# Eight of eleven down-projection steps by seven products, with a second weight sum formed early and kept in DRAM

## The chip, the core and the metric

The kernel runs on one core of one Trainium2 chip. Its engines run in parallel, each with an instruction stream of its own: TensorE (PE, with PEld for its weight loads), VectorE (DVE), ScalarE (ACT), GpSimd (POOL) and SyncE (SP, which here only issues DMAs). They meet through semaphores. The metric is device microseconds of one launch, the median of the runs shown. Weights come from DRAM by DMA and are multiplied out of on-chip tiles; sums stand in PSUM.

## The reference

One decoder layer on 16 meta tokens and 256 tokens of width 2048, in float32. The mixing part (8 retention heads, 4 mLSTM heads) is not touched by the change. What follows it is:

```python
mix = jnp.concatenate([ret, hm], axis=-1) @ w_out          # 2048 x 2048
h = h + mix
u = rmsnorm(h, norm_ffn)
up = causal_dwconv(u @ w_up, ffn_conv_w, ffn_conv_b)       # 2048 x 11264, 3 taps
gate, val = jnp.split(up, [FFN_DIM], axis=-1)              # FFN_DIM = 5632
return h + (jax.nn.silu(gate) * val) @ w_down              # 5632 x 2048
```

After it comes a last RMS norm, and the meta tokens are dropped.

## The kernel before

**Precision.** Each operand of a product is kept as a high part (float32r, a cast on ScalarE, `whi`, `sh`, `mh`) and a low part (the rest, a subtraction on VectorE, `wlo`, `sl`, `ml`). One product is three matmuls: high by high, low activation by high weight, high activation by low weight. `split` (line 763) makes both parts of a tile.

**Stages.** Input projection and heads, output projection (lines 640 to 648, 16 tiles of 128 columns in halves), then twice an up projection of 22 pairs of tiles (gate and value, lines 769 to 810) followed by the down projection of this half of the 5632 channels (lines 913 to 957). A half has `NQD` = 11 steps `q` of two channel tiles each. The 2048 output columns are four blocks of 512, taken in two pairs: `b` = 0 and 2. So there are four passes of 11 steps, one for each half and pair.

**Plain steps.** For a step and a pair the 256 tokens (two tiles) meet two channel tiles and two column blocks: eight products, done by `product` (line 814) with weights from `load_step`, into the PSUM tiles `cs[tt, j]`.

**Steps by seven products.** Steps in `FAST` do the same as a 2 x 2 block product with seven products (Winograd's form). Write the activation blocks as A11, A12, A21, A22 and the weight blocks as B11, B12, B21, B22 (channel tile, column block). The activation side forms four sums while the up projection runs: GpSimd forms S1 to S4 (lines 802 to 805), and `sh`, `sl` hold seven tiles of each step. The weight side needs four sums or differences. One of them, T = B22 - B12 + B11, is formed early: `Early` (line 600) loads three blocks into a spare buffer, `finish` does two VectorE operations and GpSimd's queue writes the 256 KB to a DRAM tile `kept`. The other three are formed in `seven` (line 830), in the down projection: it fetches T and three blocks into one of two buffers in `left` (space of the former `hT`), forms two more differences in `ta` and one in `tb` (tiles of the rotating `wraw` buffers, four of them), splits four groups of up to two blocks (`whi` and `wlo`, five buffers each) and issues 21 matmuls. Four of the seven products go to tiles `ps`, three straight to `cs`. After the last such step of a pass `share` (line 878) combines the four `ps` tiles into what each output block gets.

**Where early units run.** Five run in the output projection, at the tiles in `begins` (line 625) and in three buffers `eh`; nine in the up projection of half 0, all in the one buffer `x5`; twelve in that of half 1, in `x5` and the two `left` buffers. In the up projections a one-element operation on GpSimd (`pace`) makes the load wait for the gate tile before it. In the last pass (half 1, `b` = 2) the two steps in `BOTH` are done as plain steps; the order of its steps is written out (line 924), and the last four plain steps, `alone`, have their second block done at the very end (lines 963 to 986), so that the first token tile's final norm and store run beside the second tile's products.

**What sets the order.** A planner orders each engine's stream when the program is built, by an estimated time line; `issue_after` and `high_priority` steer it. On the chip each engine then takes its stream in order.

Of the kernel before, what the change touches and what calls it, by code (L numbers as in the profile page):

```python
# [16 lines left out]
P = 128  # L17
# [66 lines left out]
def trunk(ctx: ExitStack, tc: tile.TileContext, io, out: bass.AP):  # L84
# [509 lines left out]
    FAST = [1, 2, 3, 5, 6, 7, 8]  # L594
# [5 lines left out]
    class Early:  # L600


        def __init__(self, b, q, home, after, pace=None):

            self.home, self.age = home, 0
            self.kept = dram.tile([P, 512], F32, name=f"kept{b}_{q % NQD}", bufs=1)

            if pace is not None and after is not None:
                after = nc.gpsimd.tensor_tensor(out=pace, in0=after[:, 0:1], in1=after[:, 0:1], op=ALU.add)
            with tc.issue_after(after.ins) if after else nullcontext():  # L610
                nc.gpsimd.dma_start(home, io["wd7"][b // 2, q][:, 0:3, :])

        def finish(self, after):
            t = self.home[:, 0, :]
            with tc.issue_after(after.ins):
                nc.vector.tensor_tensor(out=t, in0=self.home[:, 1, :], in1=t, op=ALU.subtract)
            nc.vector.tensor_tensor(out=t, in0=self.home[:, 2, :], in1=t, op=ALU.add)
            nc.gpsimd.dma_start(self.kept, t)

    early, running = {}, []  # L620
    ahead = [(0, q) for q in FAST[:5]]
# [3 lines left out]
    begins = [1, 4, 6, 8, 10]  # L625
# [52 lines left out]
    def conv3(ps, f, name):  # L678
        u = wk2.tile([P, NQ], F32, name="cu", bufs=1)
        nonlocal evacuated  # L680
        evacuated = nc.vector.tensor_tensor(out=u, in0=ps[:, :NQ], in1=rstd2, op=ALU.mult)  # L681
        o = wk2.tile([P, SEQ], F32, name=name)
        nc.scalar.activation(o, u[:, 2:], AF.Identity, scale=pcol("fw", 3 * f + 2), bias=pcol("fb", f))
        for j in range(2):
            nc.vector.scalar_tensor_tensor(out=o, in0=u[:, j : j + SEQ], scalar=pcol("fw", 3 * f + j), in1=o, op0=ALU.mult, op1=ALU.add)
        return o
# [57 lines left out]
    for half in range(2):  # L744
        units = [(b, q) for b in (0, 2) for q in FAST if (half, b) != (1, 2) or q not in BOTH]
        homes = [left[0][:, 0:3, :], left[1][:, 0:3, :], x5[:, 1:4, :]]
        if half == 0:
            units = units[len(ahead):]
            begins = [2 + 4 * i for i in range(9)]
            homes = 9 * [homes[2]]  # L750
# [18 lines left out]
        for jj in range(NHF):  # L769
# [27 lines left out]
            else:  # L797
# [5 lines left out]
                nc.gpsimd.tensor_tensor(out=sums[:, S3, :], in0=e11, in1=e21, op=ALU.subtract)  # L803
# [26 lines left out]
        def seven(b, q, cs, ps, first, last, after, norm):  # L830
# [7 lines left out]
            nc.sync.dma_start(raw[:, 0, :], early[b, q])  # L838
            nc.sync.dma_start(raw[:, 1:4, :], io["wd7"][b // 2, half * NQD + q][:, 1:4, :])
            ta, tb = (wpool.tile([P, 2, 512], F32, name="wraw", bufs=4) for _ in range(2))  # L840

            nc.vector.tensor_tensor(out=ta, in0=raw[:, 0:1, :].to_broadcast([P, 2, 512]), in1=raw[:, 1:3, :], op=ALU.subtract)
            nc.vector.tensor_tensor(out=tb[:, 0, :], in0=raw[:, 3, :], in1=raw[:, 0, :], op=ALU.subtract)
            copied = None
            for w, to in (
                (raw[:, 2:4, :], ((S4, cs[0, 1], False, False), (A12, cs[0, 0], False, False))),
                (raw[:, 0:2, :], ((S2, ps[2], first, last), (A11, ps[0], first, last))),
                (ta, ((S3, ps[1], first, last), (S1, ps[3], first, last))),
                (tb[:, 0:1, :], ((A22, cs[1, 0], False, False),)),
# [11 lines left out]
            if norm:  # L861
# [4 lines left out]
                reached = nc.gpsimd.tensor_tensor(out=junk[:, 0:1], in0=tb[:, 0, 0:1], in1=tb[:, 0, 0:1], op=ALU.add)  # L866
# [49 lines left out]
        for b in (0, 2):  # L916
# [7 lines left out]
            steps = [0, 1, 4, 2, 7, 3, 5, 6, 8, 9, 10] if final else range(NQD)  # L924
# [76 lines left out]
def _layout(x, meta_tokens, norm_mix, w_in, mlstm_conv_w, mlstm_conv_b, mlstm_b_i, mlstm_b_f,  # L1001
# [30 lines left out]
    a["wd7"] = np.ascontiguousarray(np.stack([pairs[:, 1, :, :, 0], pairs[:, 0, :, :, 0], pairs[:, 1, :, :, 1], pairs[:, 0, :, :, 1]], 3))  # L1032
# [41 lines left out]
```

## Time and profile before

| | us |
|---|---|
| Median of three runs (1205.55 to 1205.96) | 1205.61 |
| The profiled execution's own time | 1205.27 |
| Its span, first to last instruction | 1203.4 |
| VectorE subtraction of a 1024-wide weight tile (line 121, 352 of them) | 1.231 |
| ScalarE cast of it (line 119, 352) | 1.050 |
| HBM read and written | 243.42 MB, 11.27 MB |

The page lists the busy time of each engine, the chain of work that ended last, and groups of instructions by line and tile. "L128" is line 128 of the kernel; `mmps<-uh,whi` names the tile written and those read, and x8 a count. In the groups of the page the up projection stands on lines 128, 129 and 131 (`mmk`), plain down-projection steps on line 828 (`product`) and seven-product steps on lines 857, 858 and 860. A matmul's listed duration overlaps the next one's, so its worth is read from start to start.

```profile
L128 PE MATMUL mmps<-uh,whi 128*128 128x258 f32 x1408 | 346.1, 283 | 0.0
...
L828 PE MATMUL atps<-whi,ml 128*128 128x512 f32 (+1 forms) x132 | 50.7, 385 | 0.0
```

Both rows end with the engine's idle time just before the group, 0.0 us: TensorE never stood before these.

### The profile page before, as it was taken

Reading aid. Unit: us, or ns where it says so; the run is one execution under the profiler, and the core shown is the slowest. Engines: PE = TensorE matmul, PEld = TensorE weight load, DVE = VectorE, ACT = ScalarE, POOL = GpSimd, SP = SyncE. Lnnn points to the kernel's source line nnn. Section 1 sums busy time; section 2 is a strip of 40 time slices with the busy share of each in tenths; the row PEclk is TensorE's granted clock in tenths of the full one; section 3 lists DMA queues with packets and bytes.
Section 4 is the critical chain, followed back from the end, with each engine's and each line's share of the span. In section 5 each row is a group of like instructions: output and inputs, shape, how many; then the busy total and the mean of one; then the engine's idle time right before and its main releaser. Section 6 shows DMA issues by size and latency. Waiting matters only on the chain.

```text
span 1203.4 us, 22768 instructions
## 1 busy us (share of the span) xinstructions
PE 1194.6 (99%) x8956; PEld 1152.1 (96%) x8956; DVE 978.2 (81%) x1458; ACT 704.2 (59%) x952; POOL 156.2 (13%) x210
## 2 busy tenths in 40 slices
PE   9999999999999999999999999999999999999997
PEld 9999999999999999999999998888999999998886
DVE  8868787766775867788989889998788778789997
ACT  8757656655656556555555556565555555556564
POOL 0100001111110311121112100101122112100131
PEclk9999999999999999999999999999999999999999
DMA  7765555566565965766866734658777677755756
GB/s 279 266 215 165 171 181 172 197 182 196 167 193 161 339 212 181 244 215 209 267 211 221 267 136 175 209 211 272 247 260 253 221 244 245 257 178 209 259 167 192
DMA packets 81275, 260.12 MB, mean 216 GB/s; under 512 B 14480, under 2 KB 18704, under 8 KB 81040
## 3 DMA queue, kind: packets, MB, share of 16 engines
q1 hardware_dynamic: 71952, 223.85, 56.3%
q0 software_dynamic: 8640, 33.96, 8.7%
q8 instruction: 70, 1.15, 0.4%
q10 hardware_dynamic: 576, 0.85, 0.2%
q14 instruction: 37, 0.30, 0.1%
HBM read 243.42 MB, written 11.27 MB: 212 GB/s over the span
## 4 chain that ended last, share of the span: by engine, by line
PE 99%; DMA 0%; SPq 0%; DVE 0%; ACT 0%; issue 0%; DVEq 0%; ACTq 0%
PE mmps L128 26%; PE mmps L129 25%; PE mmps L131 25%; PE atps L828 8%; PE mmps L858 2%; PE mmps L860 2%; PE mmps L857 2%; PE atps L858 1%; PE atps L860 1%; PE atps L857 1%; PE atps L380 1%; PE atps L372 0%; DMA wraw<-in_w 0%; PE atps L128 0%; PE atps L381 0%; PE atps L131 0%
## 5 line engine op out<-in xcount | busy, mean ns | idle before, releaser
L119 ACT CAST whi<-wraw 128x1024 fp32r<-128x1024 f32 x352 | 369.0, 1050 | 329.5 <-PE mmps L129 221.7
L121 DVE TENSOR_TENSOR wlo<-wraw,whi 128x1024 fp32r<-128x1024 f32 x352 | 432.2, 1231 | 66.5 <-ACT whi L119 63.0
L128 PE MATMUL mmps<-uh,whi 128*128 128x258 f32 x1408 | 346.1, 283 | 0.0
L129 PE MATMUL mmps<-ul,whi 128*128 128x258 f32 x1408 | 346.0, 283 | 0.0
L128 PEld LDWEIGHTS mmps<-uh,whi 128*128 128x128 f32 x1408 | 267.6, 190 | 0.1
L129 PEld LDWEIGHTS mmps<-ul,whi 128*128 128x128 f32 x1408 | 267.1, 190 | 0.1
L128 PE MATMUL mmps<-xh,whi 128*128 128x272 f32 (+2 forms) x864 | 219.9, 288 | 0.0
L129 PE MATMUL mmps<-xl,whi 128*128 128x272 f32 (+2 forms) x864 | 218.4, 286 | 0.0
L131 PE MATMUL mmps<-uh,wlo 128*128 128x258 f32 x1408 | 196.5, 282 | 0.0
L131 PEld LDWEIGHTS mmps<-uh,wlo 128*128 128x128 f32 x1408 | 179.9, 189 | 0.0
L129 PEld LDWEIGHTS mmps<-xl,whi 128*128 128x128 f32 x864 | 163.0, 189 | 0.0
L128 PEld LDWEIGHTS mmps<-xh,whi 128*128 128x128 f32 x864 | 162.6, 188 | 0.1
L131 PE MATMUL mmps<-xh,wlo 128*128 128x272 f32 (+2 forms) x864 | 126.8, 286 | 0.0
L131 PEld LDWEIGHTS mmps<-xh,wlo 128*128 128x128 f32 x864 | 114.4, 188 | 0.0
L681 DVE TENSOR_TENSOR cu<-mmps,rstd 128x258 f32<-128x258 f32 x88 | 37.4, 425 | 51.9 <-PE mmps L131 51.1
L764 ACT CAST whi<-hT 128x1024 fp32r<-128x1024 f32 x52 | 53.5, 1051 | 28.1 <-PE atps L828 8.4
L766 DVE TENSOR_TENSOR wlo<-hT,whi 128x1024 fp32r<-128x1024 f32 x52 | 62.7, 1229 | 4.9 <-ACT whi L764 3.7
L129 PE MATMUL mmps<-mixl,whi 128*128 128x258 f32 x256 | 63.0, 283 | 0.0
L128 PE MATMUL mmps<-mixh,whi 128*128 128x258 f32 x256 | 62.4, 282 | 0.0
L764 ACT CAST whi<-wraw 128x1024 fp32r<-128x1024 f32 (+1 forms) x52 | 42.9, 836 | 25.8 <-PE mmps L858 6.0
L766 DVE TENSOR_TENSOR wlo<-wraw,whi 128x1024 fp32r<-128x1024 f32 (+1 forms) x52 | 51.3, 1015 | 1.1 <-PE mmps L860 0.2
L828 PE MATMUL atps<-whi,ml 128*128 128x512 f32 (+1 forms) x132 | 50.7, 385 | 0.0
(284 smaller groups left out, 1696.7 us busy)
## 6 DMA issues: line engine op xcount, KB each, us to landing
wraw<-in_wu SPq DMA_DIRECT2D x176, 512.0 KB, 4.4
wraw<-in_wi SPq DMA_DIRECT2D x108, 512.0 KB, 4.1
hT<-in_wd SPq DMA_DIRECT2D x26, 768.0 KB, 4.7
wraw<-in_wd SPq DMA_DIRECT2D x36, 512.0 KB, 5.2
wraw<-in_wo SPq DMA_DIRECT2D x32, 512.0 KB, 4.4
x<-in_wd POOLq DMA_DIRECT2D x13, 768.0 KB, 7.2
hT<-kept SPq DMA_DIRECT2D x26, 256.0 KB, 2.7
hT<-in_wd POOLq DMA_DIRECT2D x8, 768.0 KB, 6.1
```

What stands on the lines that cost most here:

```text
L119: nc.scalar.copy(hi, raw)
L121: nc.vector.tensor_tensor(out=lo, in0=raw, in1=hi.bitcast(F32), op=ALU.subtract)
L128: nc.tensor.matmul(ps, hi[:, k, :], xh(kk), start=kk == first, stop=False)
L129: nc.tensor.matmul(ps, hi[:, k, :], xl(kk), start=False, stop=False)
L131: nc.tensor.matmul(ps, lo[:, k, :], xh(kk), start=False, stop=kk == last)
L681: evacuated = nc.vector.tensor_tensor(out=u, in0=ps[:, :NQ], in1=rstd2, op=ALU.mult)
L764: copied = nc.scalar.copy(hi, x)
L766: return copied, nc.vector.tensor_tensor(out=lo, in0=x, in1=hi.bitcast(F32), op=ALU.subtract)
L828: nc.tensor.matmul(ps, a, m[:, i, cols], start=first and n == 0, stop=seed or last and n == 5, skip_group_check=seeded)
L857: nc.tensor.matmul(o, sh[:, f, m, :], hi[:, i, :], start=begin, stop=False)
L858: nc.tensor.matmul(o, sl[:, f, m, :], hi[:, i, :], start=False, stop=False)
L860: nc.tensor.matmul(o, sh[:, f, m, :], lo[:, i, :], start=False, stop=end)
```

## The change

Of the four weight sums two are now formed early: T1 = B11 - B12 and T2 = B22 + T1, which is the T of before. An early unit loads three blocks and does two VectorE operations as before; T1, which was overwritten, is kept beside T2, and `kept` holds 512 KB a step. In `seven` the 512-column difference `tb` falls away: `ta` is (B11, B21) - T2 in one operation, (B12 - B22, B21 - T2). B22, which needs no sum, is fetched by a DMA of its own into a `wraw` tile. The order of the blocks in `wd7`, the order of the four splits and the sign of S3 follow from it.

`FAST` grows from 7 to 8 of the 11 steps. For the last pass `BOTH` becomes steps 8 and 9, and the written order of steps changes. Early units become 6 in the output projection, 10 in the first up projection, 14 in the second. To make room the value tile `vt` of the up projection has one buffer instead of two.

```diff
-    FAST = [1, 2, 3, 5, 6, 7, 8]
+    FAST = [1, 2, 3, 4, 6, 7, 8, 9]
...
-            self.kept = dram.tile([P, 512], F32, name=f"kept{b}_{q % NQD}", bufs=1)
+            self.kept = dram.tile([P, 2, 512], F32, name=f"kept{b}_{q % NQD}", bufs=1)
...
         def finish(self, after):
-            t = self.home[:, 0, :]
+            t1, t2, b11 = (self.home[:, i, :] for i in range(3))
             with tc.issue_after(after.ins):
-                nc.vector.tensor_tensor(out=t, in0=self.home[:, 1, :], in1=t, op=ALU.subtract)
-            nc.vector.tensor_tensor(out=t, in0=self.home[:, 2, :], in1=t, op=ALU.add)
-            nc.gpsimd.dma_start(self.kept, t)
+                nc.vector.tensor_tensor(out=t1, in0=b11, in1=t1, op=ALU.subtract)
+            nc.vector.tensor_tensor(out=t2, in0=t2, in1=t1, op=ALU.add)
+            nc.gpsimd.dma_start(self.kept, self.home[:, 0:2, :])
...
-    ahead = [(0, q) for q in FAST[:5]]
+    ahead = [(0, q) for q in FAST[:6]]
...
-    begins = [1, 4, 6, 8, 10]
+    begins = [1, 3, 5, 7, 9, 11]
...
-        o = wk2.tile([P, SEQ], F32, name=name)
+        o = wk2.tile([P, SEQ], F32, name=name, bufs=2 if name == "gt" else 1)
...
-            begins = [2 + 4 * i for i in range(9)]
-            homes = 9 * [homes[2]]
+            begins = [2 + 4 * i for i in range(10)]
+            homes = 10 * [homes[2]]
...
-                nc.gpsimd.tensor_tensor(out=sums[:, S3, :], in0=e11, in1=e21, op=ALU.subtract)
+                nc.gpsimd.tensor_tensor(out=sums[:, S3, :], in0=e21, in1=e11, op=ALU.subtract)
...
-            nc.sync.dma_start(raw[:, 0, :], early[b, q])
-            nc.sync.dma_start(raw[:, 1:4, :], io["wd7"][b // 2, half * NQD + q][:, 1:4, :])
-            ta, tb = (wpool.tile([P, 2, 512], F32, name="wraw", bufs=4) for _ in range(2))
-
-            nc.vector.tensor_tensor(out=ta, in0=raw[:, 0:1, :].to_broadcast([P, 2, 512]), in1=raw[:, 1:3, :], op=ALU.subtract)
-            nc.vector.tensor_tensor(out=tb[:, 0, :], in0=raw[:, 3, :], in1=raw[:, 0, :], op=ALU.subtract)
+            w = io["wd7"][b // 2, half * NQD + q]
+            nc.sync.dma_start(raw[:, 0:2, :], early[b, q])
+            nc.sync.dma_start(raw[:, 2:4, :], w[:, 2:4, :])
+            b22, ta = (wpool.tile([P, 2, 512], F32, name="wraw", bufs=4) for _ in range(2))
+            nc.sync.dma_start(b22[:, 0, :], w[:, 1, :])
+
+            nc.vector.tensor_tensor(out=ta, in0=raw[:, 2:4, :], in1=raw[:, 1:2, :].to_broadcast([P, 2, 512]), op=ALU.subtract)
             copied = None
             for w, to in (
-                (raw[:, 2:4, :], ((S4, cs[0, 1], False, False), (A12, cs[0, 0], False, False))),
-                (raw[:, 0:2, :], ((S2, ps[2], first, last), (A11, ps[0], first, last))),
-                (ta, ((S3, ps[1], first, last), (S1, ps[3], first, last))),
-                (tb[:, 0:1, :], ((A22, cs[1, 0], False, False),)),
+                (raw[:, 2:4, :], ((A11, ps[0], first, last), (A12, cs[0, 0], False, False))),
+                (raw[:, 0:2, :], ((S1, ps[3], first, last), (S2, ps[2], first, last))),
+                (b22[:, 0:1, :], ((S4, cs[0, 1], False, False),)),
+                (ta, ((S3, ps[1], first, last), (A22, cs[1, 0], False, False))),
             ):
...
-                reached = nc.gpsimd.tensor_tensor(out=junk[:, 0:1], in0=tb[:, 0, 0:1], in1=tb[:, 0, 0:1], op=ALU.add)
+                reached = nc.gpsimd.tensor_tensor(out=junk[:, 0:1], in0=ta[:, 0, 0:1], in1=ta[:, 0, 0:1], op=ALU.add)
...
-            steps = [0, 1, 4, 2, 7, 3, 5, 6, 8, 9, 10] if final else range(NQD)
+            steps = [0, 1, 5, 2, 8, 3, 4, 6, 7, 9, 10] if final else range(NQD)
...
-    a["wd7"] = np.ascontiguousarray(np.stack([pairs[:, 1, :, :, 0], pairs[:, 0, :, :, 0], pairs[:, 1, :, :, 1], pairs[:, 0, :, :, 1]], 3))
+    a["wd7"] = np.ascontiguousarray(np.stack([pairs[:, 1, :, :, 0], pairs[:, 1, :, :, 1], pairs[:, 0, :, :, 0], pairs[:, 0, :, :, 1]], 3))
```

## The prediction

> **What bounds the kernel now.** I read the page first (span, busy shares, chain), then the waits of TensorE, then the stretches in which the changed steps run.
>
> ```profile
> span 1203.4 us, 22768 instructions
> PE 1194.6 (99%) x8956; PEld 1152.1 (96%) x8956; DVE 978.2 (81%) x1458; ACT 704.2 (59%) x952; POOL 156.2 (13%) x210
> ...
> PE 99%; DMA 0%; SPq 0%; DVE 0%; ACT 0%; issue 0%; DVEq 0%; ACTq 0%
> ```
>
> The chain that ends last is TensorE for 99% of the span. What TensorE's weight loads (PEld) waited for, in all (us, times, longest):
>
> ```profile
> PEld atps L199 <- DVE ones L169: 1.1, 1, 1.1
> PEld atps L828 <- ACT whi L764: 0.4, 1, 0.4
> PEld atps L128 <- ACT whi L226: 0.3, 1, 0.3
> PEld atps L828 <- DVE hn L899: 0.3, 1, 0.3
> ```
>
> Five short waits in 1203 us (a fifth, of 0.3 us, is at the start like the first and third). Two are in the down projection, 0.7 us together. The stretches: up projection of half 0, down projection of half 0, down projection of half 1 (busy us of PE, PEld, DVE, ACT, POOL, then clock, DMA share, GB/s):
>
> ```profile
> 460.00:718.00 258.00, 258.00 (x2153) 257.94 (x2152) 218.37 (x329) 143.30 (x192) 40.57 (x57) 1.00 0.66 217
> 718.00:829.50 111.50, 111.50 (x492) 91.40 (x491) 105.56 (x113) 67.64 (x75) 3.86 (x5) 1.00 0.61 209
> 1082.60:1195.00 112.40, 112.40 (x513) 92.86 (x512) 104.73 (x116) 69.37 (x87) 21.80 (x18) 1.00 0.62 205
> ```
>
> The granted clock is 1.00. In the down stretches VectorE is busy for 95% too, so it must be asked whether TensorE is paced by its own work or by what VectorE supplies. A plain step in the chain of work, and two rows 27 matmuls apart inside a run of seven-product steps:
>
> ```profile
> 718.05 5.49 PE atps L828 x24
> ...
> 752.22 0.39 PE L857 MATMUL atps<-whi,sh 128*128 128x512 f32 x1
> ...
> 758.40 0.39 PE L857 MATMUL mmps<-whi,sh 128*128 128x512 f32 x1
> ```
>
> The plain step: 5.49 / 24 = 0.2288 us a matmul. The run: 6.18 / 27 = 0.2289 us. A plain step asks VectorE for two subtractions, a seven-product step for six operations in less time; the pace is the same. So matmuls of 512 columns set it, and one removed is worth 0.2288 us as long as supply keeps up.
>
> A rule speaks against reading it so. The Trainium skill (Perfetto Trace Analysis, Identifying the Most-Contended Engine) calls matmul busy time a poor measure of TensorE's headroom and would have the weight-load share used; here that share is 91.4 of 111.5, or 82%. Taken as a fill, it would make the removed matmuls worth 0.82 as much, some 2.25 us, and the time 1203.4. The equal pace of the two kinds of step speaks against that reading. It is the third rival below.
>
> **The matmuls.** A plain step on a pair of blocks has 2 blocks x 2 token tiles x 6 = 24 matmuls; a seven-product step has 7 x 3 = 21. FAST grows from 7 steps to 8 of 11, in half 0 for both pairs, in half 1 for pair 0; for the last pair the two steps of BOTH are plain before and after, so it grows from 5 to 6. That is four steps, each 3 matmuls shorter: 12 x 0.2288 = **2.745 us less**. No other matmul is added or dropped: 8956 become 8944.
>
> **VectorE in the down projection.** Rows of half 0, one seven-product step's start and its fetch (SPq is the DMA queue of SyncE):
>
> ```profile
> 741.17 0.33 SPq L838 DMA_DIRECT2D hT<-kept  x1
> 741.55 0.42 SPq L839 DMA_DIRECT2D hT<-in_wd  x1
> ...
> 747.59 1.23 DVE L842 TENSOR_TENSOR wraw<-hT 128x1024 f32<-128x1024 f32 x1 [0.87 <-DMA hT<-in_wd]
> ...
> 751.08 2.35 DVE L766 TENSOR_TENSOR wlo<-hT,whi 128x1024 fp32r<-128x1024 f32 x2
> 753.35 1.22 DVE L842 TENSOR_TENSOR wraw<-hT 128x1024 f32<-128x1024 f32 x1
> 754.48 0.68 DVE L843 TENSOR_TENSOR wraw<-hT 128x512 f32<-128x512 f32 x1
> 755.09 1.82 DVE L766 TENSOR_TENSOR wlo<-wraw,whi 128x1024 fp32r<-128x1024 f32 x2
> ...
> 753.46 0.33 SPq L838 DMA_DIRECT2D hT<-kept  x1
> ```
>
> From start to start a 1024-wide operation costs 1.13 us (753.35 to 754.48) and a 512-wide one 0.61 (754.48 to 755.09). A seven-product step is now 4 x 1.13 + 2 x 0.61 = 5.74 us of VectorE against 21 x 0.2288 = 4.80 of TensorE; without L843's line it is 5.13. A plain one is 2.26 against 5.49. With share and the four adds of a pair (8 x 0.61 = 4.9) a pair costs VectorE 7 x 5.74 + 4 x 2.26 + 4.9 = 54.1 of TensorE's 243 x 0.2288 = 55.6 before, and 8 x 5.13 + 3 x 2.26 + 4.9 = 52.7 of 54.9 after. The spare grows from 1.5 to 2.2 us; I count no cost. ScalarE's casts per step stay at three and a half.
>
> **The fetch of a step.** It grows from 256 + 768 KB to 512 + 512 + 256 KB, and the last is a third DMA on SyncE's queue.
>
> ```profile
> hT<-in_wd SPq DMA_DIRECT2D x26, 768.0 KB, 4.7
> wraw<-in_wd SPq DMA_DIRECT2D x36, 512.0 KB, 5.2
> hT<-kept SPq DMA_DIRECT2D x26, 256.0 KB, 2.7
> ```
>
> The first product, the new difference and the split after it need the first 1 MB, the size that is fetched now; only the third split needs the added 256 KB. From 256 to 768 KB the landing grows by 2.0 us, so 256 KB more is some 1.0 us (an estimate from these two rows) on the part used last. [...] Bounds: nothing, or the whole fetch later in the ratio of the bytes, which from 741.17 to 747.59 is 6.4 x 0.25 = 1.6 us. I take nothing: VectorE already waited 0.87 us for this fetch, and TensorE's pace at 752.22 to 758.40 shows none of it. The two buffers in `left` are given back after the same two splits as before (751.08, then 753.46 issues the next fetch). The new DMA waits for a `wraw` tile; behind it on SyncE's queue stands the next step's fetch. But that tile is the one of two steps back, while the next fetch needs `left` from one step back, which is free later. So it adds no wait.
>
> **Early units, before the down projection.** There are 30 instead of 26, each with the same two 512-wide operations on VectorE (1.2 us) and 512 KB written instead of 256. VectorE is busy 218 of 258 us in the up projection, with TensorE at 258.00: the work lies beside it. The crowded place is the output projection, where the first five run as early as their buffers allow:
>
> ```profile
> 395.00:405.00 10.00, 10.00 (x86) 10.00 (x85) 10.00 (x15) 6.83 (x11) 5.65 (x6) 1.00 0.94 317
> 405.00:415.00 10.00, 10.00 (x86) 10.00 (x86) 9.80 (x12) 3.83 (x7) 3.70 (x6) 1.00 0.95 337
> ...
> ACT whi L119 <- DMA wraw<-in_wo: 4.5, 5, 1.4
> ```
>
> One unit more (768 + 512 KB) and five writes 256 KB longer are 2.6 MB, at 337 GB/s some 7.8 us more of full DMA queues. ScalarE waited five times for weights here, 1.4 us at most, and TensorE never. Between no cost and 1.4 us (one more such wait reaching TensorE) I take none. The second `vt` buffer goes:
>
> ```profile
> 718.55 0.60 ACT L683 ACTIVATE vt<-cu,par 128x256 f32<-128x256 f32 x1 [0.32 <-DVE cu L681]
> ...
> 720.59 0.43 DVE L788 TENSOR_TENSOR gt<-gt,vt 128x256 f32<-128x256 f32 x1
> ```
>
> The tile is read 2.0 us after it is written, and written again two projections later: 96 matmuls at 258 / 2153 = 0.12 us, 11.5 us. The new wait of ScalarE, with the casts behind it, is met by far. Sign changes on GpSimd and the order inside `wd7` cost nothing.
>
> **The sum.** 2.745 us less and nothing added. The profiled execution took 1205.27 us (span 1203.4): 1202.5, span 1200.7. The median shown is 0.34 us above it: 1205.61 - 2.745 = **1202.87 us**. A measurement of this kernel tells 0.2% (2.4 us) from no change, so the forecast is just beyond it, and anything above 0.33 us given back turns it into "same".
>
> **Rivals.** *The boundary between pairs gives back (0.20).* Between the last seven-product step of a pair and the first of the next lie steps 9, 10 and 0 now, step 10 and 0 after. VectorE has to do there the subtractions, share, the adds and the next step's first pieces: now 6.8 + 4.9 + 2.9 = 14.6 us in 3 x 5.49 = 16.5, after 4.5 + 4.9 + 2.3 = 11.7 in 11.0. It is short by 0.7 us, to be met from its lead. The one wait of 0.4 us on ScalarE above is at such a boundary (773 us), after a load came late:
>
> ```profile
> 766.46 1.05 ACT L119 CAST whi<-wraw 128x1024 fp32r<-128x1024 f32 x1 [2.84 <-DMA wraw<-in_wd]
> ```
>
> Against it: the other boundary (1130 to 1140) lost nothing. Price 0.7 us at each of two: 1204.3.
>
> *The tail gives back (0.16).* In the last pair steps 8, 9, 10 follow the last seven-product step now, 9 and 10 after.
>
> ```profile
> 1176.58 0.39 PE L860 MATMUL atps<-wlo,sh 128*128 128x512 f32 x1
> ...
> 1195.32 0.40 PE L828 MATMUL atps<-wlo,mh 128*128 128x256 f32 x2
> ...
> 1190.58 0.68 DVE L899 TENSOR_TENSOR hn<-atps,hn 128x512 f32<-128x512 f32 x1
> 1195.76 0.15 DVE L705 TENSOR_SCALAR rest<-rest 128x1 f32<-128x1 f32 x1
> ...
> 1178.44 1.05 ACT L119 CAST whi<-wraw 128x1024 fp32r<-128x1024 f32 x1 [2.62 <-DMA wraw<-in_wd]
> ...
> 1196.09 0.19 ACT L985 ACTIVATION_READ_ACCUMULATOR junk<-atps 128x1 f32 x1
> ```
>
> TensorE needs 18.7 us from there to its end, 16.0 after. VectorE's chain (share, four adds, first half's norm) ends at 1195.91, ScalarE's end of the second half at 1196.28: 0.37 us to spare. If that chain keeps its length, 2.4 us are lost; it has one load's subtraction less (1.13), so 1.2: 1204.1. For it: the chain is dense. Against it: 2.6 us of its start are a wait for a weight load, and with one load less ahead the loads come sooner against the end; the first product of share is now in a step's first split.
>
> *Supply, not matmuls, sets the pace (0.03)*: the removed matmuls turn into bubbles and lose between 18% of their worth (what the weight loads leave of the down stretch, 20.1 of 111.5 us) and all of it: 1203.4 to 1205.6.
>
> *Fetches starve the runs of four (0.08), slower.* In 1-4 and 6-9 the third and fourth step are fetched only when the first and second give back their buffers.
>
> ```profile
> 747.68 1.05 ACT L764 CAST whi<-hT 128x1024 fp32r<-128x1024 f32 x1
> 749.22 1.06 ACT L764 CAST whi<-hT 128x1024 fp32r<-128x1024 f32 x1 [0.49 <-PE atps L858]
> ```
>
> These casts wait for TensorE to free a buffer, so they are the five buffers ahead: at 747.68 about one step, 4.8 us, is still to be multiplied. The low part is needed four matmuls (0.9 us) after that, at 753.4; VectorE had it at 751.08 + 1.22 = 752.3. That leaves 1.1 us, and 1.7 once L843's 0.61 is gone. If the larger fetch lands later than that by 1 us (2.7 in all, beyond the bound of 1.6, with the queues full of writes), 1 us reaches TensorE in each of seven runs of four: 7 us, less 2.7: 1209.9. It decides above 1.7 us of delay. Against it: steps 5-8 are such a run already, and no wait of TensorE is shown in it.
>
> **Chances.** Forecast 0.53, boundary 0.20, tail 0.16, bubbles 0.03, starving 0.08. Faster by over 0.2%: 0.53; same: 0.20 + 0.16 + 0.03 = 0.39; slower: 0.08. The range goes from 1202.0 (both waits of the down projection gone, 0.7 us, and rounding) to 1204.8 (boundary or tail, with half a us for either being mis-sized); it leaves out the starving case and the tail at its full 2.4 us.
>
> **What would show it.** 8944 matmuls; the down stretch of half 0 1.4 us shorter at 0.229 us a matmul; TensorE's waits still under 1 us in all; VectorE's busy time there some 3 us lower; HBM writes up by 30 x 0.52 - 26 x 0.26 = 8.9 MB. A PEld wait on `whi` or `wlo` near a pair's end shows the boundary, ScalarE's last square long after the last matmul the tail, a wait on `hT<-kept` in every third or fourth step the starving. A time above 1205.6 proves the argument wrong.

## The result: 2.2% slower, and the profile after

| | median us (lowest to highest) | runs |
|---|---|---|
| before, on the same chip | 1205.78 | 4 |
| changed | 1232.22 (1227.82 to 1234.55) | 4 |
| ratio, 95% interval | 1.0216 (1.0204 to 1.0229) | |

The change was forecast to take 2.7 us off; it added 26.4. The execution profiled after the change took 1233.17 us, with a span of 1231.3. From its page, in the order span, busy time by engine, HBM traffic, chain of work that ended last:

```profile
span 1231.3 us, 22885 instructions
...
PE 1203.2 (98%) x8944; PEld 1149.8 (93%) x8944; DVE 977.5 (79%) x1454; ACT 704.9 (57%) x962; POOL 175.2 (14%) x229
...
HBM read 254.43 MB, written 20.19 MB: 223 GB/s over the span
...
PE 4%; DMA 2%; DVE 1%; ACT 0%; issue 0%; DVEq 0%; ACTq 0%; SPq 0%
```

The 8944 matmuls and the written bytes are as the prediction had them. But the chain is no longer TensorE from end to end: it can be followed over only 7% of the span, through weight loads (DMA) and VectorE. TensorE is busy for longer although it does fewer matmuls: a matmul is listed with 0.39 us, of which 0.2288 count where the next one follows at once and all 0.39 ahead of a stop, and the clock fell at times (last section). So busy time hides the loss, and the count of matmuls in a stretch shows it (columns: window, its length, busy us of PE, PEld, DVE, ACT, POOL with counts, clock, DMA share, GB/s). First the up projection of half 0, then the down projection of half 0 (two rows) and of half 1 (two rows); the first, second and fourth windows are as long as those shown of before.

```profile
460.00:718.00 258.00, 258.00 (x2152) 257.90 (x2152) 215.62 (x325) 139.28 (x190) 46.50 (x64) 1.00 0.70 233
718.00:829.50 111.50, 107.05 (x453) 85.03 (x452) 98.96 (x103) 68.89 (x78) 3.54 (x4) 0.98 0.68 223
829.50:838.00 8.50, 8.50 (x48) 7.35 (x47) 6.62 (x9) 5.63 (x6) 0.00 (x0) 1.00 0.87 292
1090.50:1202.90 112.40, 100.09 (x411) 76.96 (x410) 95.06 (x98) 64.50 (x79) 15.36 (x14) 0.97 0.67 219
1202.90:1222.80 19.90, 19.20 (x103) 15.41 (x101) 16.98 (x27) 10.62 (x18) 5.32 (x5) 1.00 0.63 178
```

Up to 718 us nothing is lost. In the window in which the down projection of half 0 did 492 matmuls it now does 453; in half 1, 411 instead of 513. From its first matmul to its last, the down projection of half 0 takes 118.0 us instead of 111.4 (2 and 12 matmuls of the next up projection that lie between, 0.12 us each, taken off), that of half 1 with the end of the kernel 132.6 instead of 113.2 (up projections between and before them: +1.6 and -0.2). Nearly all of the loss is in the down projections, three quarters of it in half 1. What TensorE's matmuls waited for, and what its weight loads (PEld) waited for (us, times, longest):

```profile
PE mmps L858 <- ACT whi L764: 7.0, 4, 3.8
PE atps L861 <- DVE wlo L766: 4.2, 2, 4.0
PE mmps L861 <- DVE wlo L766: 3.6, 3, 1.3
PE atps L828 <- ACT whi L119: 2.6, 8, 0.4
...
PEld mmps L858 <- ACT whi L764: 9.1, 5, 4.2
PEld mmps L861 <- DVE wlo L766: 7.3, 10, 1.7
PEld atps L828 <- ACT whi L119: 6.0, 8, 0.9
PEld atps L861 <- DVE wlo L766: 5.9, 5, 4.4
```

The matmuls waited 17.4 us for the high and low parts of weights in the down projections, where before none waited. The weight loads, which the prediction's rows are about, waited 28.3 us, where before there were two waits of 0.7 us together, one of them for a weight part. ScalarE and VectorE are not busier than before (VectorE 977.5 us after 978.2). So they were late because they waited themselves, and two places show for what.

**The start of the down projection of half 1**, from the timeline (start, duration, engine, line, operation, out<-in, and in brackets the wait ahead of it):

```profile
1088.47 0.68 DVE L616 TENSOR_TENSOR hT<-hT 128x512 f32<-128x512 f32 x1
...
1090.50 0.39 PE L828 MATMUL atps<-whi,mh 128*128 128x512 f32 x1
...
1091.18 0.58 POOL L618 DMA_DIRECT2D kept<-hT  x1 [7.66 <-DVE hT L617]
...
1095.66 0.33 SPq L839 DMA_DIRECT2D hT<-kept  x1
...
1101.14 1.23 DVE L844 TENSOR_TENSOR wraw<-hT 128x1024 f32<-128x1024 f32 x1 [4.02 <-DMA hT<-kept]
1102.29 0.42 DVE L681 TENSOR_TENSOR cu<-mmps,rstd 128x258 f32<-128x258 f32 x1
...
1103.36 0.50 PE L861 MATMUL atps<-wlo,sh 128*128 128x512 f32 x1 [4.00 <-DVE wlo L766]
...
1104.92 0.63 PE L859 MATMUL mmps<-whi,sl 128*128 128x512 f32 x1
1105.35 0.63 PE L858 MATMUL atps<-whi,sh 128*128 128x512 f32 x1
```

Read it from the top. The last early unit of half 1 is finished at 1088.47, hardly ahead of the first matmul of the down projection, and its sums leave its home only with the write at 1091.18. This home (the spare buffer of a unit) is the second buffer of `left`: the list of homes has three entries, and with fourteen units instead of twelve the last falls on another entry. So the fetch of the second seven-product step waits until 1095.66, VectorE stands at L844 for it until 1101.14, and TensorE stops for 4 us. Behind L844 stands, too, the reading of the last projection's sum (L681 at 1102.29), twelve us after TensorE had left that projection: VectorE was late already.

**VectorE's waits in the up projections**, in all, after and then before (L844 is `ta` in the down projection, which before waited 0.9 us, once):

```profile
DVE x L616 <- DMA x<-in_wd: 30.9, 11, 6.0
DVE hT L616 <- DMA hT<-in_wd: 27.5, 9, 5.2
...
DVE wraw L844 <- DMA hT<-kept: 19.8, 11, 4.0
...
DVE cu L681 <- PE mmps L131: 8.2, 8, 1.5
```

```profile
DVE cu L681 <- PE mmps L131: 51.1, 51, 1.5
...
DVE hT L616 <- DMA hT<-in_wd: 7.2, 3, 4.4
...
DVE x L616 <- DMA x<-in_wd: 4.0, 5, 1.2
```

Before, VectorE waited 51 times for a projection to end (L681): it ran ahead. Now it does so 8 times, and instead waits 58.4 us for the loads of early units (L616), 11.2 before. A unit's load starts when GpSimd's `pace` has seen a `gt`, and a `gt` is late when VectorE is: late loads and a late VectorE keep each other going. A lag does TensorE little harm in the up projections (one stop of 1.3 us, at 1000 us), but it is what the down projection starts with.

**The end of a pair** in the down projection of half 1, where two runs of seven-product steps meet:

```profile
1148.04 0.33 SPq L840 DMA_DIRECT2D hT<-in_wd  x1
...
1149.17 0.33 SPq L839 DMA_DIRECT2D hT<-kept  x1
...
1149.77 1.46 SPq L116 DMA_DIRECT2D wraw<-in_wd  x2
...
1158.61 1.04 ACT L119 CAST whi<-wraw 128x1024 fp32r<-128x1024 f32 x1 [3.98 <-DMA wraw<-in_wd]
...
1161.94 0.77 PE L858 MATMUL mmps<-whi,sh 128*128 128x512 f32 x1 [3.79 <-ACT whi L764]
```

The plain loads of step 0 are issued behind the next pair's first fetches and land almost nine us later. All casts of ScalarE are one line, so the cast of the next seven-product step, whose matmul is next in TensorE's line, stands behind this one, and TensorE stops for 3.8 us. The same happened in half 0 near 776 us (2.5 us; a stop for which no row is shown is measured from start to start of two matmuls, less 0.2288 us).

### The profile page after: what moved, and what is told of

It reads as the page before. It is cut to its first block, busy times and chain, and to the rows that moved or that the text cites. A ratio compares the mean times of both kernels' runs of the same rounds, so it can differ in the third digit from the quotient of the medians.

```text
span 1231.3 us, 22885 instructions
## 1 busy us (share of the span) xinstructions
PE 1203.2 (98%) x8944; PEld 1149.8 (93%) x8944; DVE 977.5 (79%) x1454; ACT 704.9 (57%) x962; POOL 175.2 (14%) x229
## 5 line engine op out<-in xcount | busy, mean ns | idle before, releaser
L119 ACT CAST whi<-wraw 128x1024 fp32r<-128x1024 f32 x344 | 358.9, 1047 | 269.1 <-PE mmps L129 125.4
L121 DVE TENSOR_TENSOR wlo<-wraw,whi 128x1024 fp32r<-128x1024 f32 x344 | 424.3, 1235 | 72.2 <-ACT whi L119 70.8
L131 PEld LDWEIGHTS mmps<-xh,wlo 128*128 128x128 f32 x864 | 114.2, 188 | 0.0
L766 DVE TENSOR_TENSOR wlo<-hT,whi 128x1024 fp32r<-128x1024 f32 x60 | 71.4, 1218 | 1.5 <-PE atps L828 1.3
L764 ACT CAST whi<-hT 128x1024 fp32r<-128x1024 f32 x60 | 61.7, 1049 | 15.9 <-PE atps L859 5.0
L764 ACT CAST whi<-wraw 128x512 fp32r<-128x512 f32 (+1 forms) x60 | 49.3, 834 | 25.9 <-DVE wlo L766 18.0
L766 DVE TENSOR_TENSOR wlo<-wraw,whi 128x512 fp32r<-128x512 f32 (+1 forms) x60 | 58.2, 1006 | 0.0
L858 PE MATMUL mmps<-whi,sh 128*128 128x512 f32 x120 | 48.5, 404 | 7.0 <-ACT whi L764 7.0
L844 DVE TENSOR_TENSOR wraw<-hT 128x1024 f32<-128x1024 f32 x30 | 37.7, 1258 | 20.0 <-DMA hT<-kept 19.8
```

The lines of the kernel that those rows point to most:

```text
L119: nc.scalar.copy(hi, raw)
L121: nc.vector.tensor_tensor(out=lo, in0=raw, in1=hi.bitcast(F32), op=ALU.subtract)
L131: nc.tensor.matmul(ps, lo[:, k, :], xh(kk), start=False, stop=kk == last)
L764: copied = nc.scalar.copy(hi, x)
L766: return copied, nc.vector.tensor_tensor(out=lo, in0=x, in1=hi.bitcast(F32), op=ALU.subtract)
L844: nc.vector.tensor_tensor(out=ta, in0=raw[:, 2:4, :], in1=raw[:, 1:2, :].to_broadcast([P, 2, 512]), op=ALU.subtract)
```

## Experiments

All times are medians with the lowest and highest run; the kernel before was run beside each set and gave 1204.85 to 1205.67. Ratios are to it.

| run | us | ratio, 95% interval |
|---|---|---|
| n7 | 1207.88 (1205.43 to 1210.19) | 1.0017 (1.0007 to 1.0026) |
| o8 | 1224.14 (1223.50 to 1224.53) | 1.0151 (1.0136 to 1.0166) |
| home | 1222.62 (1218.85 to 1225.62) | 1.0137 (1.0116 to 1.0159) |
| ord | 1234.03 (1232.15 to 1235.08) | 1.0232 (1.0217 to 1.0247) |
| borrow | 1215.65 (1213.94 to 1218.34) | 1.0085 (1.0068 to 1.0102) |
| dummy | 1208.85 (1205.79 to 1215.54) | 1.0037 (1.0018 to 1.0056) |
| homeage | 1213.74 (1213.11 to 1215.19) | 1.0069 (1.0054 to 1.0084) |
| row8 | 1212.96 (1210.46 to 1216.15) | 1.0062 (1.0041 to 1.0084) |
| all | 1213.10 (1212.39 to 1214.74) | 1.0063 (1.0048 to 1.0078) |
| third | 1221.66 (1217.85 to 1229.23) | 1.0140 (1.0102 to 1.0179) |
| all3 | 1210.48 (1209.16 to 1212.16) | 1.0040 (1.0025 to 1.0055) |
| all3b | 1212.40 (1210.99 to 1215.61) | 1.0064 (1.0045 to 1.0084) |
| borrow3 | 1211.33 (1210.76 to 1214.92) | 1.0055 (1.0038 to 1.0072) |
| row3 | 1207.74 (1206.23 to 1212.02) | 1.0024 (1.0012 to 1.0036) |
| mid3 | 1214.59 (1212.28 to 1215.65) | 1.0079 (1.0062 to 1.0096) |
| midq | 1217.05 (1216.42 to 1218.10) | 1.0094 (1.0077 to 1.0111) |
| rowq | 1212.27 (1210.65 to 1214.95) | 1.0058 (1.0042 to 1.0074) |
| midb | 1217.86 (1217.19 to 1218.42) | 1.0107 (1.0090 to 1.0124) |

### The two halves of the change, each alone: n7 and o8

The change has two parts: a new form of a step (two sums prepared and kept instead of one), and an eighth step in the form. n7 has the form with the seven steps, their places and the units' order of before; o8 has eight steps in the old form.

```diff
n7:  FAST = [1, 2, 3, 5, 6, 7, 8], begins and steps as before, vt with two buffers
o8:  kept of one block, three operations per unit and per step as before; FAST = [1, 2, 3, 4, 6, 7, 8, 9]
```

> New form (T1 and T2 kept, 512 KB, three fetches a step) with the old seven steps, old begins, old order of steps and two vt buffers. If the larger fetch itself starves the steps, this is slow as well: 26 of the 30 steps are fetched so, about 20 us lost, 1225. If the eighth step's consequences (home of the last early unit, one plain step fewer between runs) cost it, this is within 2 us of 1205.8.

> Old form (T alone kept, 256 KB, one difference more on VectorE) with eight steps, the new begins and order of steps and one vt buffer. If the larger fetch is to blame: 1203 to 1206. If the eighth step's consequences are: the last early unit again sits in a left buffer, so TensorE again waits 4 us or more at the start of the second down projection, and the time is 1215 to 1230.

n7 costs 2.2 us against the kernel before on its chip (1205.65), o8 18.5. By itself the form is a small part; the eighth step is the large one. Together these are 20.7 of the 26.4 us: beside eight steps the form costs 8.1 us (1232.2 against 1224.1), not 2.2. In n7 VectorE waits 9.7 us for fetches (six times) where before waited 0.9 us, but TensorE's stops are three of 0.3 to 0.4 us.

### Units or pair: borrow and dummy

The eighth step brings two things: more early units (30 instead of 26), and eight seven-product steps in a pair. Each was tried without the other: eight steps with the old units (borrow), seven steps with the new units (dummy). In borrow step 9 (in the last pass step 7) uses the kept sums of the step before, so its output lacks the right part of these steps.

```diff
borrow:
+    SEVEN = [q for q in FAST if q != 9]
-    ahead = [(0, q) for q in FAST[:6]]
+    ahead = [(0, q) for q in SEVEN[:5]]
...
-            nc.sync.dma_start(raw[:, 0:2, :], early[b, q])
+            nc.sync.dma_start(raw[:, 0:2, :], early[b, q if (b, q) in early else q - 1])
dummy (to n7, with the begins of the change):
-        units = [(b, q) for b in (0, 2) for q in FAST if ...]
+        units = [(b, q) for b in (0, 2) for q in FAST + [9] if ...]
```

> The changed kernel with the early units of the kernel before (5 in the output projection, 9 and 12 in the up projections); the steps without a unit of their own multiply another step's kept sums, so their part of the output is left out. All eight steps run by seven products. Theory A (the added early units and where the last ones sit make the load, not the eighth step in the down projection): VectorE's lag in the up projections falls back below 1 us, the stop of 4 us at the start of the down projection of half 1 goes, and the time is at most 1212 us. Theory B (the eighth step in the pair itself costs: the end of a pair, the order inside a step): the stops at the ends of the pairs stay and the time is 1218 us or more.

> The opposite of the run before: the new form with seven steps by seven products (1207.9 us with its own early units), with the early units of the changed kernel: 6, 10 and 14, of which one in eight prepares sums that no step reads. Theory A: 1218 us or more, with VectorE's lag in half 1 at 4 us or more and a wait for a kept sum or its buffer at the start of the down projection of half 1. Theory B: at most 1211 us.

With n7 and the changed kernel they make a square:

| | old units | new units |
|---|---|---|
| seven steps | 1207.9 | 1208.9 |
| eight steps | 1215.7 | 1232.2 |

Neither theory holds alone. The added units cost 1 us beside seven steps (though two of dummy's ten runs took over 1215 us) and 16.6 beside eight. The eighth step costs 7.8 us beside the old units, and 10.5 against what its matmuls should save. The rows of the square differ in two more things, the buffers of `vt` (two beside seven steps) and the order of the last pass; no run varies these alone.

The crossing shows in the traces before the second down projection starts. In the up projection of half 1 VectorE reads a sum this long after the projection's last matmul, on average: 0.1 us in n7, 2.1 in dummy, 0.6 in borrow, 6.7 in the changed kernel. With eight steps VectorE enters this stage 2.7 us late (borrow and the changed kernel), with seven 0.2 us at most. Beside the old units it has caught up after some ten projections, although borrow has one `vt` buffer, too; beside the new ones it falls further behind, to 11.6 us at the last. That a pair of seven steps also takes up more of a lag than one of eight is argued, not shown.

### Where the units cost: home and homeage

home moves the last unit of half 1 to the block that no early fetch needs; homeage also finishes a unit of half 1 one projection later, so that VectorE doesn't come to it before its load.

```diff
-            homes = 5 * homes
+            homes = 5 * [homes[1], homes[2], homes[0]]
homeage, too:
-                if running and running[0].age == 2:
+                if running and running[0].age == 2 + half:
```

> The changed kernel with one edit: the three buffers of the early units in the second up projection in another turn, so that the last unit uses x5 and both left buffers are free some 20 us before the down projection. Theory of the home: the fetch no longer waits 4.9 us for a kept write, TensorE's 4.2 us stop at 1099 us goes with the 1 us behind it and a stretch at half clock (1.7 us): 5 to 8 us faster, 1225. Rival (lag of VectorE alone): under 2 us.

> The run with other homes in half 1 (1222.6 us), with the unit of half 1 finished three projections after its load instead of two. If VectorE lags because it stands waiting for the units' loads at the head of its line, the lag in half 1 falls from 5 us to below 2 us and the time by 3 to 8 us, to 1215 to 1220. If the lag is only a sign of full transfer queues, or does not reach the down projection, the time stays within 2 us of 1222.6.

home takes 9.6 us off, and its profile has no stop near 1099 us any more. homeage takes off another 8.9. In the profiled executions half 1's down projection, from first to last matmul, takes 132.6 us in the changed kernel, 125.2 in home and 115.7 in homeage; half 0's, which these edits leave alone, 118.2, 119.6 and 118.4. VectorE's waits in homeage:

```profile
DVE cu L681 <- PE mmps L131: 40.7, 41, 1.5
...
DVE x L616 <- DMA x<-in_wd: 7.8, 8, 3.8
...
DVE hT L616 <- DMA hT<-in_wd: 2.3, 3, 1.6
```

VectorE is ahead of TensorE again (41 waits for a projection's end), and 10.1 us of waits for loads stand where 58.4 stood. The two edits give back 18.5 us, about what the square has for the units (16.6). That the units' loads at the head of VectorE's line, and one home, were what the units cost in half 1 is thereby shown. Half 0's loss of some 6 us stays.

### Order inside a step: ord

The difference `ta` stands at the head of a step on VectorE and waits for the fetch, with older splits behind it. ord forms it after both raw splits.

```diff
+                if w is ta:
+                    with tc.issue_after(parted.ins):
+                        nc.vector.tensor_tensor(out=ta, in0=raw[:, 2:4, :], ...)
```

> The changed kernel with ta formed after both splits of a step's raw blocks are on VectorE's stream, so that the subtraction that frees the buffers no longer stands behind an operation that waits for the next fetch. Theory of the order: waits of ta for kept fall from 19.8 to under 6 us, and TensorE's stops of 0.3 to 1.5 us inside the runs go: 6 to 10 us faster, 1223. Rival (fetch too slow in itself): no change, 1232.

A miss: 1234.0 us. VectorE's waits for kept sums, 19.8 us in the changed kernel, are gone, but `ta`'s product is now late itself: its matmuls wait for its cast in 18 of the 30 steps (one of the 19 waits is for another cast):

```profile
PE mmps L859 <- ACT whi L764: 21.3, 19, 1.8
```

This order only moves the loss; another one was not tried.

### What the eighth step costs in the pair: row8 and all

row8 (to home) lets the eight steps follow one another, so that three plain steps lie between pairs as before the change. all has this and the later finish of homeage.

```diff
-    FAST = [1, 2, 3, 4, 6, 7, 8, 9]
+    FAST = [1, 2, 3, 4, 5, 6, 7, 8]
-            steps = [0, 1, 5, 2, 8, 3, 4, 6, 7, 9, 10] if final else range(NQD)
+            steps = [0, 1, 7, 2, 8, 3, 4, 5, 6, 9, 10] if final else range(NQD)
```

> The run with other homes (1222.6 us), with steps 1 to 8 by seven products, so that three plain steps (9, 10, 0) lie between two pairs as in the kernel before, and eight seven-product steps follow one another. If the end of the pair is what costs (stops of 2.7 us near 778 us and 3.6 us near 1151 us, with a halved clock behind them), these go and the time falls by 5 to 9 us, to 1214 to 1218. If the fetches starve a long run of such steps, new waits for a kept sum stand in the run and the time is 1222 us or more.

> Other homes, units of half 1 finished three projections after their load, and steps 1 to 8 by seven products, together. Each of the last two took 8.9 and 9.7 us from 1222.6 us. If they are separate losses they add: 1222.6 - 8.9 - 9.7 = 1204 us. If both only give VectorE a lead that the run of seven-product steps then uses up (the same loss twice), 1210 to 1213 us, with TensorE's stops left in the second half of each run.

row8 takes 9.7 us off home: the stops at the end of a pair (2.7 and 3.6 us) are gone. But all is no faster than row8 or homeage. The losses do not add. My reading is that a lead of VectorE (weights ready ahead of TensorE) is of use once, and the long run uses up what there is. One turn of that run in row8 (SyncE's queue, VectorE, TensorE):

```profile
747.54 0.33 SPq L839 DMA_DIRECT2D hT<-kept  x1
...
751.56 0.33 SPq L839 DMA_DIRECT2D hT<-kept  x1
...
756.59 1.22 DVE L844 TENSOR_TENSOR wraw<-hT 128x1024 f32<-128x1024 f32 x1 [1.05 <-DMA hT<-kept]
758.98 0.33 SPq L839 DMA_DIRECT2D hT<-kept  x1
...
759.00 0.74 PE L861 MATMUL mmps<-wlo,sh 128*128 128x512 f32 x2 [1.52 <-DVE wlo L766]
```

The fetches use two buffers in turn, so the first and the third line use the same one: 11.4 us for two steps, 5.7 a step, where TensorE needs 4.80. VectorE waits 1.05 us for the fetch issued at 751.56, and TensorE 1.52 for VectorE. In the first pair of each half all turns from the fourth fetch on take 11.0 to 11.4 us. The kernel before had slower ones without a stop (14.3 us, from 726.89 to 741.17, in its run of four steps), so a slow turn seems to cost only where the run outlasts the lead.

### A third buffer: third, all3, row3

The four blocks of `x5` are idle in the down projection until share fills them at a pair's end. They are made a third buffer for fetches; in row3 for the fourth and seventh step of a pair only. (In the runs the caller hands the buffer to `seven`; the lines below say which one.)

```diff
-            raw = left[turn]
-            turn = 1 - turn
third (to the change), all3 (to all):
+            raw = (left[0], left[1], x5)[fast.index(q) % 3]
row3 (to all):
+            raw = (left[0], left[1], left[0], x5, left[1], left[0], x5, left[1])[fast.index(q)]
```

> The changed kernel (1232.2 us) with a third buffer for the fetches of the seven-product steps (the four blocks that hold share's results at a pair's end), nothing else. If the two buffers pace a run of such steps (two steps in 11.1 us against TensorE's 9.6), the pace falls to TensorE's and the time by 8 us or more, to at most 1224 us. If the losses come from the up projections alone (the lag and the last unit's home), the time stays within 3 us of 1232.

> The three edits together and the third buffer. Theory of the two buffers: no stop of TensorE over 0.5 us is left in the runs of eight, and the time is 1202 to 1205 us. Rival (VectorE's order inside a step or the mass of bytes paces the run, not the buffers): within 1.5 us of the run without the third buffer.

> The three edits together with the third buffer (1210.5 us), the buffer given to the fourth and seventh step of a pair instead of the third and sixth, so that no fetch waits for share's results to leave it. The two stops of 2.35 and 1.46 us early in the second pair go: 1205 to 1208 us. If the fetch there is late for another reason, the same within 1 us.

By itself the third buffer gives 10.6 us of the change's loss back. On top of the other edits it gives 2.6, and 5.4 once no fetch has to wait for share's results to leave `x5`. row3, at 1207.74 us, is the fastest form of the change found: 24.5 of the 26.4 us lost are back. From all to row3 the down projection of half 0 falls from 117.1 to 114.2 us, that of half 1 from 116.2 to 113.6 (profiled executions, first to last matmul; before 112.8 and 113.2). Row3's waits of matmuls in the down projections:

```profile
PE atps L827 <- ACT whi L119: 0.9, 2, 0.5
...
PE mmps L857 <- DVE wlo L765: 0.2, 1, 0.2
```

Its weight loads still waited 7.0 us there, 1.0 at the longest. Against the kernel before it is 1.0012 to 1.0036 times as long: nothing tried here beats that kernel.

### Misses: all3b, borrow3, mid3, midq, rowq, midb

all3b is all3 with the later finish in half 0, too (`age == 3`). mid3 is homeage, with its two runs of four, and row3's buffers; borrow3 is borrow with them. midq and rowq take the loads of the plain steps off SyncE's queue; midb (to mid3) gives the fourth block of a fetch buffers of its own, in half 1 alone.

```diff
midq, rowq:
-            return load_w(io["wd"][b, half * NQD + q], [P, 2, 512], to)
+            return load_w(..., to, nc.sync if q == 0 or half == 1 and b > 1 else nc.gpsimd)
midb:
-            b22, ta = (wpool.tile([P, 2, 512], F32, name="wraw", bufs=4) for _ in range(2))
+            b22 = ... if half == 0 else more.tile([P, 1, 512], F32, name="b22", bufs=2)
+            ta = wpool.tile([P, 2, 512], F32, name="wraw", bufs=4)
```

> The run before with the units of half 0, too, finished three projections after their load. If VectorE's lag at the end of the up projection of half 0 (about 2 to 5 us) is what starts the down projection of half 0 late, that stretch is 0.5 to 2 us shorter and the time lower by as much; otherwise the same within 0.5 us.

> The run with the early units of the kernel before (1215.7 us; steps without a unit of their own multiply another step's kept sums, so their part of the output is left out), with a third buffer for the fetches of the seven-product steps, given to the fourth and the seventh step of a pair. If the two buffers are the whole of what the eighth step in a pair costs, TensorE's stops go with them and the time is 1202 to 1206 us. If VectorE's own pace in a run (5.1 us a step against 4.8) or the plain step's late loads hold it, 1208 us or more.

> Other homes and the later finish (1213.7 us), steps as in the change (two runs of four), with the same third buffer. Buffers as the cause: the plain step between two runs lets VectorE catch up, so it is as fast as or faster than the run of eight, 1203 to 1207 us. If the loads of the plain step stand too late behind the fetches, its stops of 2 us near 768 and 802 us stay and the time is 1209 us or more.

> The run with two runs of four steps and the third buffer (1214.6 us, with stops of 2.55 us at 798.5 and 1.23 us at 1140 before plain steps), with the loads of the plain steps 5 and 10 issued from GpSimd's queue instead of SyncE's, except in the last pair and step 0. If those loads come late because they stand behind the fetches on SyncE's line, they are issued earlier, the stops go, and the time falls to 1204 to 1209 us. If they come late because their buffer or the queues are late, within 2 us of 1214.6.

> The same edit to the run of eight steps with the third buffer (1207.7 us), for steps 9 and 10. TensorE's waits for a plain load's cast there are 2.3 us in all: 1205 to 1207 us if SyncE's line is what holds the loads, 1207 to 1209 us if not.

> The run with two runs of four steps and the third buffer (1214.6 us, loads on SyncE's queue), where in half 1 alone the fourth block of a fetch (b22) has two buffers of its own and no longer takes one of the four wraw buffers that the plain loads use. If these buffers are what makes the plain loads late, half 1's down projection, 117.1 us from the end of its up projection to the last matmul, falls below 115 us and the time to 1210 to 1212 us, with half 0 unchanged. If not, 117 us and 1214 to 1215 us.

all3b gained nothing: VectorE's lag in half 0 (from a projection's last matmul to the reading of its sum, on average) was 2.6 us with the edit and 1.9 without, and it differs by more than that between kernels planned alike there (0.7 in third, 2.0 in the changed kernel). borrow3 took 4.3 us off borrow, not the 10 that the buffers alone would explain; a stop of 3.0 us before the lone plain step 5 is left. mid3 has the same stop (2.55 us near 799) and is no faster than homeage, which has two buffers, and slower than row3's run of eight by 6.9 us. rowq was slower than row3 by 4.5 us. midq was to show that SyncE's line holds those loads. It was slower, and GpSimd stood at the load as well:

```profile
798.50 0.56 POOL L116 DMA_DIRECT2D wraw<-in_wd  x1 [16.06 <-DVE wlo L765]
```

It waited for VectorE's split that frees a `wraw` buffer, and the cast of what it fetched came 4.7 us later. That pointed to the four `wraw` buffers, of which the fourth block of each fetch now holds one from its transfer on. midb frees them, and was slower by 3.3 us: the loads were then issued up to 15 us ahead, the planner put the casts in another order, and a stop of 2.8 us near 1142 stood where one of 1.2 had been. So why the lone plain step's loads are late is not settled: SyncE's line is ruled out as the only cause, the buffers are neither shown nor ruled out.

## Why the prediction was wrong, step by step

**Matmuls and their pace.** 8944, and 0.2288 us each where nothing waits: right. The condition, "as long as supply keeps up", is what failed. I read from equal pace in two kinds of step that supply keeps up; over 27 matmuls equal pace showed only that nothing was late in these, not how much lead was left.

**Early units.** "The work lies beside it" is the step that failed most. VectorE's busy time in the up projection of half 0 even fell (215.6 us of 258 after 218.4); its waits grew. I counted operations and bytes, and placed the crowd in the output projection. What counted was in the up projections: VectorE takes a unit's load in its own order, so a load that is late by up to 6 us holds everything behind it. Waits for such loads went from 11.2 to 58.4 us. And the last unit moved from `x5` to a buffer of `left`, which a list that I had read would have told. Together they cost 16.6 us (borrow) to 18.5 us (home and homeage) beside eight steps. The single `vt` buffer ("met by far") was not varied alone; borrow and homeage have it and are not late (0.6 and 0.7 us in half 1).

**The fetch of a step.** "I take nothing" and "it adds no wait" failed too. The form costs 2.2 us beside seven steps (n7), 8.1 beside eight (o8), and in the changed kernel VectorE waited for `hT<-kept` in 11 of 30 steps, which is the sign named for starving.

**Fetches starve the runs of four.** The rival with the right sign, and in kind the right mechanism: with two buffers a turn took 5.7 us a step. I gave it 0.08 and a price of 7 us. As the sole mechanism it was mis-sized: the third buffer alone returned 10.6 us, the two edits of the units 18.5, and these overlap (24.5 with all in row3). Nor was the larger fetch, its condition, the main thing: o8 lost 18.5 us with the old one.

**Boundary between pairs.** I priced VectorE's work there, 0.7 us at each of two. The stops were 2.5 and 4.0 us (start to start), from plain loads that landed late and from the single line of casts behind them; an engine's sum of work did not show it.

**The tail.** Stops of 0.4 to 0.55 us after 1198 us, 1.4 us in all; it was not what decided.

**VectorE in the down projection.** Its work did fall. A window round each down projection, before and then in row3:

```profile
717.90:831.30 113.40, 113.40 (x505) 93.11 (x504) 107.36 (x116) 68.79 (x76) 4.78 (x6) 1.00 0.62 210
1082.50:1195.50 113.00, 113.00 (x518) 93.46 (x516) 104.73 (x116) 69.94 (x89) 21.80 (x18) 1.00 0.63 206
```

```profile
717.70:832.50 114.80, 113.89 (x499) 91.40 (x498) 104.85 (x109) 72.58 (x80) 3.88 (x5) 1.00 0.71 228
1083.70:1197.00 113.30, 112.74 (x512) 91.96 (x511) 103.81 (x112) 72.67 (x92) 20.86 (x18) 1.00 0.71 225
```

In half 0 it falls by 2.5 us, where I had some 3. That was right, and it was worth less than it seemed: less work lets VectorE come sooner to a fetch that is no sooner there. Even in row3 the down projections are 1.4 and 0.4 us longer than before, from first to last matmul, where their matmuls alone would make both 1.4 us shorter.

**The range** left out every case above 1204.8 us: I took each cover one at a time ("met by far", "lies beside") and never asked what happens if two thin covers are used by the same lateness. The square above is that case.

## What to carry to other kernels

Where two engines are both over 90% busy, ask how much lead the second has and what each added wait at the head of its line does to it, before counting the work that it saves. When a list of buffers is dealt out in turn, one entry more changes who holds which buffer at the next stage: write down the last holder of each. Try a change's two halves alone and crossed; two costs of 1 and 8 us were 24 together here.

## What the runs showed of the hardware

TensorE's clock was granted at half rate for a while after some of the stops. The timeline above has it: behind the 4 us stop matmuls of 512 columns are listed with 0.63 us instead of 0.39, and the one at 1105.35 starts 0.43 us after the one at 1104.92, where 0.2288 is the pace. Behind the stop at 1158 us, by stretches of 10 us:

```profile
1150.00:1160.00 10.00, 7.51 (x31) 5.19 (x29) 5.98 (x7) 3.73 (x5) 0.00 (x0) 1.00 0.75 267
1160.00:1170.00 10.00, 8.06 (x28) 6.38 (x29) 10.00 (x13) 6.41 (x7) 3.51 (x4) 0.83 0.75 171
```

A mean clock of 0.83 over 10 us is 1.7 us of lost clock; three such drops before the last matmul of the changed kernel make up to 5 of its 26.4 us (an estimate: where TensorE stands during a drop, less is lost). At half rate the 1.7 us are a drop of 3.4 us. The Trainium skill (TensorE: Matmul & The Clock Gate, HAM oscillation) asks that TensorE have no gaps over about 3.4 us. The drop here is as long as that figure, but as a limit on gaps the figure doesn't hold: a stop of 1.98 us in homeage, at 768 us, was followed by such a drop, and one of 2.73 us in third, at 787 us, was not (one stretch of each):

```profile
766.00:776.00 10.00, 8.18 (x29) 6.24 (x28) 7.82 (x9) 4.05 (x5) 0.00 (x0) 0.83 0.87 322
```

```profile
785.00:795.00 10.00, 7.44 (x33) 5.51 (x32) 5.72 (x6) 5.74 (x7) 0.00 (x0) 1.00 0.73 256
```
